# Moving the split of u in front of a drive in the gate stage of a hybrid RG-LRU / HGRN2 layer

## The chip, the cores and the metric

The kernel runs on one core of one Trainium2 chip. The metric is the device time of one execution in microseconds (us); a run's time is the median of several executions. Five engines work side by side, each through its own instructions in a fixed order, and wait for each other by semaphores: PE (TensorE, matmuls), ACT (ScalarE), DVE (VectorE), POOL (GpSimd) and SP (which issues most DMAs).

## What is computed

One layer for 512 latent tokens and 256 context tokens, 2048 wide. A normalised, modulated input h is multiplied by one wide input matrix. Its columns feed two groups, a gated linear recurrence (RG-LRU, 16 blocks of 128 channels) and a HGRN2 group; both outputs, gated, go through an output matrix. Only the RG-LRU group is touched by the change. For each block:

```python
ua = dwconv_centred(xa, conv_w, conv_b)            # 4 taps
r = sigmoid(ua @ w_r + b_r)                        # per block, per direction
i = sigmoid(ua @ w_i + b_i)
log_a = -8.0 * r * softplus(-lam)
a = exp(log_a)
bx = sqrt(-expm1(2.0 * log_a)) * (i * ua)
h = linear_scan(a, bx, h0)                         # context first, then latent
ya = (h_fwd + flip(h_bwd)) * silu(ga)
```

## The kernel before

The input product is made in units of 128 columns: h stands still in SBUF as 16 pairs of tiles (a rounded part `h` and its remainder, both in a format that PE takes at full rate), and the weights stream through `wraw`, six buffers deep. For each weight block ACT rounds it into `whi` (line 146), POOL makes the remainder `wlo` (line 147), and PE multiplies `whi` with both parts of h and `wlo` with the first (`mm_unit`, lines 204, 205 and 207). Five buffers of `whi` and `wlo` stand between ACT, POOL and PE.

The first stage, up to about 630 us, makes the columns of the RG-LRU group, two units per block of channels: xa and ga. Here a block of 128 channels is called a head, h = 0 to 15. The elementwise work and the gate products of a head are cut into small steps that stand in a queue `wq`; after every second weight slice of the main product a credit decides whether the next one or two steps are written into the program. So the order of all instructions on every engine is fixed when the program is built.

`steps_a(h)` (from line 357) makes the 13 steps of a head, in two lists, `first` and `second` (lines 457 and 458):

- `conv_a`, `conv_b`: the convolution of four taps into `u`; the first tap on ACT (line 369), the others on DVE (line 371). `u` has one buffer, so the first tap of the next head waits until POOL has read the last one's u (line 416).
- `split`: ACT rounds u into `uh` (line 390), and DVE subtracts, `ul = u - uh` (line 391).
- `g2(0)`, `g2(1)`: for each direction two gate products on PE (lines 402 and 403, six matmuls each, of `uh`, `ul` and `uh`), into two PSUM banks per product out of four banks `w`; then two sigmoids on ACT (lines 406 and 407) into the tiles `r` and `i`. `g2(0)` takes all four banks, and so `g2(1)` waits on PE until ACT has read them.
- `tanh`: two activations on ACT, and the product i*u on POOL, in place (line 416, twice).
- `exp`, `sqrt`: two activations each on ACT (lines 420 and 424), each pair behind a load of an activation table.
- `drive(d)`: two DVE instructions on `s` for direction d (lines 429 and 430); the first needs the square root of that direction.
- `scan(d)`: two scans on DVE (lines 439 and 441), over context (`hc`) and latent tokens (`hl`), which read `r` of the direction, now holding a.
- `fin`: the sum of both directions and the product with the gate on DVE, and the DMA of the result.

`r` and `i` have two buffers each, one per direction. So a sigmoid of `g2(0)` of head h overwrites the buffer that `scan(0)` of head h - 1 reads, and waits for that scan.

`push_a` puts the steps of a head together with the second list `p` of the preceding head. Written by their names, the order before is: conv_a(h), exp(h-1), conv_b(h), sqrt(h-1), drive(0)(h-1), split(h), scan(0)(h-1), drive(1)(h-1), scan(1)(h-1), g2(0)(h), fin(h-1), g2(1)(h), tanh(h). Where the text says "the cycle of head h", it means these 13 steps.

Of the kernel before, what the change touches and what calls it, by code (L numbers as in the profile page):

```python
# [56 lines left out]
def layer_kernel(ctx: ExitStack, tc, xT, xres, w0, w0e, wi, adas, adag, adagb, wo, par, lw, fw, cst, masks, out):  # L57
# [405 lines left out]
    def push_a(h):  # L463
        f, n = steps_a(h)
        if prev:
            p = prev.pop()
            f = [f[0], p[0], f[1], p[1], p[2], f[2], p[3], p[4], p[5], f[3], p[6], f[4], f[5]]
        wq.extend(f)
        prev.append(n)
        if h == NH - 1:  # L470
            wq.extend(prev.pop())
# [5 lines left out]
    e, a, n2, s2, p, m = (sm[:, i, :] for i in range(6))  # L477
# [45 lines left out]
    for h in range(2):  # L523
        evac_ga(h, PG[h])
        push_a(h)
# [337 lines left out]
    for i in range(NP):  # L863
# [13 lines left out]
        if i < 4 * NA:  # L877
            u, g = divmod(i, 4)
            cb = ORDER_A[u]
            full = cb < 16  # L880
            if g == 0:
                ph = psm.tile([128, 2, 512], F32, name="m")
            for k in range(4):
                mm_unit(ph if full else ph[:, 1, :], hi[:, k, :], lo[:, k, :], 4 * g + k, full)
                if k % 2:
                    credit += 1.5 if full else 1.0
                    while credit >= 1.33:
                        credit -= 1.33
                        run_steps(1)
            if g == 3:  # L890
                if cb >= 16:
                    evac_ga(cb - 16, ph[:, 1, :])
                else:
                    evac_xa(cb, ph[:, 0, 0:C], ph[:, 1, :])
                    push_a(cb)
            continue
# [190 lines left out]
```

## Time and profile before

| what | value |
|---|---|
| median of 3 runs | 2274.55 us (2274.06 to 2274.7) |
| the profiled execution, its own time | 2273.24 us |
| its span in the trace | 2271.5 us |
| PE busy | 2238.4 us, 99% of the span |
| DVE busy | 1233.7 us, 54% |
| ACT busy | 1014.5 us, 45% |
| POOL busy | 954.4 us, 42% |

Busy time says how long an engine had an instruction in it; it does not say what that engine waited for, nor that the others have room at each moment. The trace gives for each instruction its start, its duration and, in square brackets, how long its engine stood idle ahead of it and which instruction ended that idle time. A duration can hold a wait too: an instruction that has started but cannot get at its data is shown as long.

### The profile page before, as it was taken

The numbers are of one execution on the slowest core, as the hardware profiler recorded it, in microseconds if no ns is written. First come the engines' busy times: TensorE is split into PE (matmuls) and PEld (weight loads), VectorE is DVE, ScalarE is ACT, GpSimd is POOL, SyncE is SP. The second block draws the span as 40 slices with busy tenths as digits, with TensorE's granted clock in tenths as the row PEclk, the third lists the DMA queues.
The fourth block names the chain that finished last, engine by engine and source line by source line (L and its number), as shares of the span: only waits on it lengthen the run. The fifth ranks groups of instructions, "written<-read, shape, count | busy, mean of one in ns | idle before, by whom it ended". The sixth has DMA issues, their size and how long they took to land.

```text
span 2271.5 us, 40504 instructions
## 1 busy us (share of the span) xinstructions
PE 2238.4 (99%) x16318; PEld 1915.5 (84%) x16318; DVE 1233.7 (54%) x1834; ACT 1014.5 (45%) x1845; POOL 954.4 (42%) x698
## 2 busy tenths in 40 slices
PE   8999999999999999999999999999999999999998
PEld 4788888888898898898898898998998987788886
DVE  5447666665645666565576566556646647610011
ACT  4357767777634343343334334334334334422222
POOL 2355555565532433433333234234424334455452
PEclk9999999999999999999999999999999999999999
DMA  9942222222222323323223223223223224553443
GB/s 365 361 152 84 80 84 84 84 94 79 70 75 78 86 80 89 89 76 88 76 86 91 69 83 98 80 71 94 80 66 107 76 70 127 176 162 97 125 122 110
DMA packets 121396, 242.05 MB, mean 107 GB/s; under 512 B 13812, under 2 KB 16244, under 8 KB 121208
## 3 DMA queue, kind: packets, MB, share of 16 engines
q1 hardware_dynamic: 118520, 231.06, 32.9%
q0 software_dynamic: 2688, 8.40, 1.1%
q8 instruction: 128, 2.10, 0.4%
q14 instruction: 60, 0.49, 0.1%
HBM read 226.81 MB, written 12.59 MB: 105 GB/s over the span
## 4 chain that ended last, share of the span: by engine, by line
PE 92%; DVE 3%; issue 2%; ACT 2%; POOL 0%; DMA 0%; SPq 0%; ACTq 0%; DVEq 0%; POOLq 0%
PE m L205 22%; PE m L207 21%; PE m L204 12%; PE m L857 8%; PE w L975 8%; PE m L975 6%; PE w L857 4%; PE w L403 2%; PE w L685 2%; PE w L207 2%; PE w L769 2%; PE w L273 1%; PE w L402 1%; PE w L786 1%; PE w L785 1%
## 5 line engine op out<-in xcount | busy, mean ns | idle before, releaser
L147 POOL TENSOR_TENSOR wlo<-wraw,whi 128x512 fp32r<-128x512 f32 x556 | 793.4, 1437 | 1070.5 <-ACT whi L146 1013.6
L205 PE MATMUL m<-h,whi 128*128 128x512 f32 x1536 | 572.3, 395 | 0.0
L146 ACT CAST whi<-wraw 128x512 fp32r<-128x512 f32 x556 | 340.0, 620 | 457.2 <-issue 121.4
L207 PE MATMUL m<-h,whi 128*128 128x512 f32 x1440 | 448.1, 392 | 0.0
L204 PE MATMUL m<-h,whi 128*128 128x256 f32 x1536 | 437.9, 285 | 0.0
L205 PEld LDWEIGHTS m<-h,whi 128*128 128x128 f32 x1536 | 288.3, 188 | 63.7 <-issue 0.5
L207 PEld LDWEIGHTS m<-h,whi 128*128 128x128 f32 x1440 | 268.1, 188 | 55.8 <-issue 0.5
L205 PE MATMUL m<-h,wlo 128*128 128x512 f32 x768 | 303.6, 395 | 0.0
L204 PEld LDWEIGHTS m<-h,whi 128*128 128x128 f32 x1536 | 290.1, 189 | 8.9 <-issue 6.2
L207 PE MATMUL m<-h,wlo 128*128 128x512 f32 x720 | 280.9, 390 | 0.0
L204 PE MATMUL m<-h,wlo 128*128 128x256 f32 x768 | 216.2, 282 | 0.0
L857 PE MATMUL m<-whi,h 128*128 128x256 f32 x1024 | 207.8, 286 | 0.0
L658 DVE TENSOR_TENSOR KK<-KK,T 128x768 f32<-128x768 f32 x112 | 142.5, 1273 | 109.2 <-PE w L685 77.5
L205 PEld LDWEIGHTS m<-h,wlo 128*128 128x128 f32 x768 | 144.0, 188 | 35.1
L857 PEld LDWEIGHTS m<-whi,h 128*128 128x128 f32 x1024 | 168.5, 191 | 1.2 <-issue 0.2
L207 PEld LDWEIGHTS m<-h,wlo 128*128 128x128 f32 x720 | 135.2, 188 | 28.5
L590 DVE STREAM_TRANSPOSE ktok<-KK 32x384 f32<-32x384 f32 x256 | 145.9, 570 | 3.5
L371 DVE SCALAR_TENSOR_TENSOR u<-xp,P,u 128x256 f32<-128x256 f32 x96 | 88.2, 978 | 104.9 <-ACT u L369 104.9
L204 PEld LDWEIGHTS m<-h,wlo 128*128 128x128 f32 x768 | 145.0, 189 | 0.0
L857 PE MATMUL m<-wlo,h 128*128 128x256 f32 x512 | 144.8, 283 | 0.0
L638 ACT COPY Kc<-KK 128x512 f32<-128x512 f32 x80 | 54.6, 682 | 182.0 <-DVE KK L658 129.3
L776 DVE SCALAR_TENSOR_TENSOR S<-S,T,w 128x128 f32<-128x128 f32 x128 | 44.5, 348 | 134.9 <-ACT S L774 71.7
(222 smaller groups left out, 3762.1 us busy)
## 6 DMA issues: line engine op xcount, KB each, us to landing
wraw<-in_wi SPq DMA_DIRECT2D x428, 256.0 KB, 2.7
araw<-in_adas SPq DMA_DIRECT2D x64, 512.0 KB, 7.3
wraw<-in_wo SPq DMA_DIRECT2D x128, 256.0 KB, 2.7
wraw<-in_adag SPq DMA_DIRECT2D x64, 256.0 KB, 2.7
y_d<-ys POOLq DMA_DIRECT2D x32, 256.0 KB, 2.8
wraw<-y_d SPq DMA_DIRECT2D x32, 256.0 KB, 3.2
h<-in_xT SPq DMA_DIRECT2D x16, 384.0 KB, 7.4
wraw<-in_w SPq DMA_DIRECT2D x16, 256.0 KB, 7.9
```

The source lines that it names most:

```text
L146: act.copy(hi, t)
L147: pool.tensor_sub(lo, t, hi.bitcast(F32))
L204: pe.matmul(ph[:, 0, 0:C], w, h[:, 0:C], start=s, stop=e)
L205: pe.matmul(ph[:, 1, :], w, h[:, C:TA], start=s, stop=e)
L207: pe.matmul(ph, w, h[:, C:TA], start=s, stop=e)
L371: dve.scalar_tensor_tensor(dst, xp[:, o + k:o + k + n], cw, dst, op0=ALU.mult, op1=ALU.add)
L403: pe.matmul(pl, w[:, i, :], x[:, C:TA], start=n == 0, stop=n == 2)
L590: dve.transpose(dst[32 * j:32 * j + 32, :, 32 * i:32 * i + 32], src[32 * i:32 * i + 32, :, 32 * j:32 * j + 32])
L638: act.copy(Kc[l].rearrange("p c n -> p (c n)").rearrange("p (a b c) -> p a b c", b=2, c=m), view(s["K"], C, [[2 * m, C // m], [TA + m, 2], ...
L658: dve.tensor_mul(kk, kk, view(Tm, 1, [[2, nb // 2], [nb - 1, 2], [0, m]]))
L857: pe.matmul(o, x[:, 128 * j:128 * j + 128], wlin(w)[:, 256 * k:256 * k + 256], start=kb == 0 and n == 0 and j % 2 == 0, stop=kb == KB - 1 ...
L975: pe.matmul(pos[tk], y[:, 128 * tk:128 * tk + 128], wlin(x), start=(kb == 0 and n == 0), stop=(kb == 2 * KB - 1 and n == 2))
```

## The change

In `push_a` the step `f[2]` (split of head h) moves one place to the front, ahead of `p[2]` (drive of the first direction of head h - 1). Nothing is added or removed.

```diff
-            f = [f[0], p[0], f[1], p[1], p[2], f[2], p[3], p[4], p[5], f[3], p[6], f[4], f[5]]
+            f = [f[0], p[0], f[1], p[1], f[2], p[2], p[3], p[4], p[5], f[3], p[6], f[4], f[5]]
```

The order of the instructions on PE, POOL and SP stays the same. On DVE and ACT it changes as follows.

On DVE, in the cycle of head 7, ahead of the scan of the first direction (L371 are the taps of u, L429 and L430 the drive, L391 the remainder of u, L439 and L441 the scans). Before:

```order
L371 SCALAR_TENSOR_TENSOR u<-xp_1386,P,u 128x512
L429 SCALAR_TENSOR_TENSOR s<-r,s 128x768
L430 TENSOR_TENSOR s<-s,i 128x768
L391 TENSOR_TENSOR ul<-u,uh 128x768
L439 SCALAR_TENSOR_TENSOR hc<-r,s 128x256
L441 SCALAR_TENSOR_TENSOR hl<-r,hc,s 128x512
```

And now, at the same place:

```order
L371 SCALAR_TENSOR_TENSOR u<-xp_1386,P,u 128x512
L391 TENSOR_TENSOR ul<-u,uh 128x768
L429 SCALAR_TENSOR_TENSOR s<-r,s 128x768
L430 TENSOR_TENSOR s<-s,i 128x768
L439 SCALAR_TENSOR_TENSOR hc<-r,s 128x256
L441 SCALAR_TENSOR_TENSOR hl<-r,hc,s 128x512
```

The remainder of u stands ahead of both drive instructions now; this is so in the cycles of all heads from 1 to 15.

On ACT, in the cycle of head 7 (L424 are the square roots, L146 a weight block, L390 the rounding of u, L323 and L324 the evacuation of the next xa), as a difference of the two orders:

```order
 L424 ACT_TABLE_LOAD
 L424 ACTIVATE s<-s 128x768 x2
-L146 CAST whi<-wraw 128x512
-L390 CAST uh<-u 128x768
+L390 CAST uh<-u 128x768
+L146 CAST whi<-wraw 128x512
 L323 COPY xp_1386<-m 128x256
 L324 COPY xp_1386<-m 128x64x8
```

The rounding of u changes places with one weight block. On ACT this happens in the cycles of heads 1, 4, 5, 7, 8, 9 and 10; in the others the order of ACT is unchanged.

On DVE, in the cycle of head 10, with buffer numbers (gsa is the gate, which waits for a sigmoid of ACT):

```order
+L391 TENSOR_TENSOR ul_4190<-u_4128,uh_4189 128x768
+L354 TENSOR_TENSOR gsa_4195<-m_4097,sg_4193 128x512
 L429 SCALAR_TENSOR_TENSOR s_4104<-r_4019,s_4104 128x768
 L430 TENSOR_TENSOR s_4104<-s_4104,i_4030 128x768
-L354 TENSOR_TENSOR gsa_4193<-m_4097,sg_4191 128x512
-L391 TENSOR_TENSOR ul_4215<-u_4128,uh_4214 128x768
 L439 SCALAR_TENSOR_TENSOR hc_4230<-r_4019,s_4104 128x256
```

Here the drive now stands behind the gate product as well.

## Rows read from the trace of the kernel before

**Rows 1.** PE's waits, 200 to 640 us: us in total, times, longest.

```profile
PE w L402 <- DVE ul L391: 1.5, 3, 0.7
PE w L402 <- ACT r L406: 0.9, 1, 0.9
```

**Rows 2.** Waits of ACT, 130 to 640 us, same columns.

```profile
ACT r L406 <- PE w L402: 35.4, 11, 5.8
...
ACT u L369 <- POOL i L416: 30.8, 11, 4.5
...
ACT r L406 <- DVE hl L441: 22.0, 9, 4.5
ACT L406 <- DVE hl L441: 21.4, 6, 4.6
```

**Rows 3.** Timeline of ACT, head 7: start, us, instruction [idle before <-releaser].

```profile
354.35 1.58 ACT L424 ACTIVATE s<-s 128x768 f32<-128x768 f32 x2
355.83 0.61 ACT L146 CAST whi<-wraw 128x512 fp32r<-128x512 f32 x1
356.35 0.83 ACT L390 CAST uh<-u 128x768 fp32r<-128x768 f32 x1
...
363.12 1.28 ACT L406 ACT_TABLE_LOAD   x1 [3.75 <-DVE hl L441]
364.41 0.47 ACT L406 ACTIVATE r<-w,P 128x256 f32<-128x256 f32 x1
```

**Rows 4.** Timeline of DVE, head 7.

```profile
355.23 0.96 DVE L429 SCALAR_TENSOR_TENSOR s<-r,s 128x768 f32<-128x768 f32 x1 [1.83 <-ACT s L424]
...
357.21 1.94 DVE L391 TENSOR_TENSOR ul<-u,uh 128x768 fp32r<-128x768 f32 x1
...
360.88 2.14 DVE L441 TENSOR_TENSOR_SCAN hl<-r,hc,s 128x512 f32<-128x512 f32 x1
```

**Rows 5.** Timeline of POOL, head 7.

```profile
356.57 1.76 POOL L147 TENSOR_TENSOR wlo<-wraw,whi 128x512 fp32r<-128x512 f32 x1 [2.02 <-ACT whi L146]
358.99 2.95 POOL L147 TENSOR_TENSOR wlo<-wraw,whi 128x512 fp32r<-128x512 f32 x2 [0.66 <-ACT whi L146]
```

**Rows 6.** Timeline of PE, heads 7 and 15: first matmul of the second gates.

```profile
364.94 0.38 PE L402 MATMUL w<-uh,lhi 128*128 128x256 f32 x1 [0.94 <-ACT r L406]
...
604.79 0.28 PE L402 MATMUL w<-uh,lhi 128*128 128x256 f32 x1
```

**Rows 7.** Timeline of ACT, heads 3, 5 and 15.

```profile
238.39 0.83 ACT L390 CAST uh<-u 128x768 fp32r<-128x768 f32 x1
...
251.21 0.47 ACT L406 ACTIVATE r<-w,P 128x256 f32<-128x256 f32 x1 [3.77 <-PE w L402]
...
299.19 0.84 ACT L390 CAST uh<-u 128x768 fp32r<-128x768 f32 x1
...
603.69 0.47 ACT L406 ACTIVATE r<-w,P 128x256 f32<-128x256 f32 x1 [3.02 <-DVE hl L441]
```

**Rows 8.** Timeline of DVE, heads 3, 5 and 10.

```profile
237.28 0.96 DVE L429 SCALAR_TENSOR_TENSOR s<-r,s 128x768 f32<-128x768 f32 x1 [1.78 <-ACT s L424]
...
249.38 1.28 DVE L441 TENSOR_TENSOR_SCAN hl<-r,hc,s 128x512 f32<-128x512 f32 x1
...
296.37 0.96 DVE L429 SCALAR_TENSOR_TENSOR s<-r,s 128x768 f32<-128x768 f32 x1 [1.32 <-ACT s L424]
300.06 0.96 DVE L391 TENSOR_TENSOR ul<-u,uh 128x768 fp32r<-128x768 f32 x1 [1.74 <-ACT uh L390]
300.93 1.77 DVE L439 TENSOR_TENSOR_SCAN hc<-r,s 128x256 f32<-128x256 f32 x1
...
444.29 0.69 DVE L354 TENSOR_TENSOR gsa<-m,sg 128x512 f32<-128x512 f32 x1 [0.69 <-ACT sg L352]
...
446.93 1.77 DVE L439 TENSOR_TENSOR_SCAN hc<-r,s 128x256 f32<-128x256 f32 x1
```

## The prediction

> **What bounds the kernel now.** By the table of busy times PE is at work for 99% of the span, so only time in which PE stands idle can be won, and any new idle time of PE is lost. I looked first at what PE waits for in the gate stage, since the change lies there. In the sum of waits PE waits for ul, the remainder of u, in 3 places for 1.5 us, and for a sigmoid of the gates in one place for 0.9 us [rows 1]; no other line of that list is longer than half a microsecond. If the 2.4 us vanished, the kernel would gain 0.1%, less than the 0.2% that a measurement of it can tell from no change. The change can't win much; what has to be read is what it can lose.
>
> That is seen on the side of the other engines. The sum of ACT's waits has the sigmoids (L406, and the table load ahead of them) held by the scan hl of DVE 15 times, 43.4 us in all, and the first tap of u held by POOL's product i*u 11 times, 30.8 us; the 11 other waits of the sigmoids are for PE [rows 2]. Placed in time, nearly all the waits for PE lie in heads 0, 2 and 3 and again from head 11 on, and the waits for the scan lie in heads 4 to 10 and in 15. So from head 4 to head 10 the steps form a ring that hardly waits for PE: sigmoid, tanh, i*u on POOL, first tap of u, exp, square root, drive, scan, sigmoid of the next head. In these heads PE is the one who waits. Head 7 shows it: DVE starts the drive as soon as ACT has the first square root (355.23, after 1.83 us idle) and then works without a pause up to the end of hl at 363.02 (360.88 + 2.14) [rows 4]; ACT, idle for 3.75 us, loads its table at 363.12 and starts the sigmoid at 364.41 [rows 3]; PE had been idle for 0.94 us when the bank came free, and starts the second gates at 364.94 [rows 6]. A delay anywhere in that ring goes to PE, and the next head starts from there.
>
> **The change part by part.** No instruction is added or taken away, and no queue but those of DVE and ACT has another order; the DMAs of weights and results stay where they are. Two things move.
>
> First, the rounding of u goes ahead of one weight block on ACT in seven heads. It costs PE nothing by itself: that block comes 0.83 us later at most, the length of the rounding [rows 3], under the cover of the other buffers of whi, and no wait of PE for whi shows in this stage.
>
> Second, DVE does ul ahead of the drive. The drive needs only the first square root; ul needs both square roots and the rounding behind them on ACT. Before, DVE did the two drive instructions (0.96 us each) in just that time, and found uh ready [rows 4]. Now it stands idle. In head 7 the roots end at 355.93 (354.35 + 1.58), the rounding 0.83 later, at 356.76 at the latest [rows 3], where the drive had started at 355.23 [rows 4]. DVE's string of work is the same but starts 1.5 us later. Queued behind ul on DVE: drive and scan of the first direction, then of the second; for these wait the sigmoids, for them PE's second gates and the next head's u.
>
> What POOL does within that string is part of the price. The row of ul is 1.94 us, that of head 5 0.96 [rows 4, 8]; the long one began at 357.21, while POOL had its wlo open from 356.57 to 358.33 [rows 5]: the two took turns. The three wlo blocks of this stretch come as before or 0.8 us later, and POOL's next block starts at 358.99, within ul, and ends later than its own length: it gets in between two DVE instructions again [rows 5]. So I take it that the same wlo blocks still fall into the string, and give neither gain nor loss for them.
>
> Now head by head, each against before:
> - Head 3 brings the ring in late. Its rounding isn't moved and ends at 239.22 (238.39 + 0.83) [rows 7]; the drive had begun at 237.28, so the string starts 1.97 late, and the second hl, which ended at 250.66 (249.38 + 1.28), ends at 252.63 [rows 8]. The sigmoid that began at 251.21, waiting for PE [rows 7], now waits for that scan: +1.5.
> - Heads 4, 6, 7, 8, 9 show the pattern of head 7: +1.5 each, 7.5. (In 6 the rounding follows the roots already; in the others it does so now.)
> - Head 5: ul was waited for before, 1.74 us, until 300.06 [rows 8]. The rounding, one weight block (0.61 less their overlap of 0.1) earlier [rows 3], starts near 298.68 instead of 299.19 and ends near 299.52 [rows 7]; then ul 0.96, and the drive, 1.95, that used to lie in DVE's idle time: the scan starts near 302.45 instead of 300.93 [rows 8], +1.5; with one wlo block within the drive, 1.1 more. I take +2.0.
> - Head 10: the drive is now behind the gate gsa too, which waits for ACT's sigmoid; the rounding ahead of it puts gsa from 444.29 to about 445.04, its end at 445.73, and two drive instructions later it is 447.65 instead of 446.93 [rows 8]: +0.7, with a wlo block +1.8. I take +1.2.
> - Sum: 1.5 + 7.5 + 2.0 + 1.2 = 12.2. In heads 7 and 10 PE waited for the sigmoid before, so nothing is left to hide it: PE is 12.2 us late behind head 10.
> - Heads 11 to 14: the sigmoids wait for PE, 3.2 us on average over the 11 such waits [rows 2], and a string up to 1.97 late costs PE nothing. Head 1, which starts without a delay carried in, isn't in the sum either.
> - Head 15: as in head 3 the rounding isn't moved on ACT, and the string starts 1.97 late. The sigmoid ended at 604.16 (603.69 + 0.47), and PE came at 604.79, so 0.63 of it is covered [rows 6, 7]: +1.3. (The ring is not closed here; this head waits for the scan, but the heads ahead of it for PE.)
> - What is gained: the waits of PE for ul go, since ul comes 1 us earlier. But PE then only comes sooner to the second gates and waits there, in heads 5, 7 and 9, where these waits lay. I give it nothing.
>
> The sum is 13.5 us. Behind the gate stage PE has next to no idle time until the output product, and there it works at the same things as before: nothing gives the time back. Against the profiled execution's own time, 2273.24, this is 2286.7; the median of the runs is 1.3 above that execution, so 2274.55 + 13.5 = 2288.
>
> **The rivals.**
> *The ring catches up.* If a delay weren't carried from head to head (because something ahead of the first tap has room that the waits don't show), each head would pay for itself: 1.5 less its own cover. Heads 4 and 8 would pay nothing, 7 its full 1.5, 5 and 10 about 1.4 each, 15 its 1.3, 6 and 9 a few tenths each: about 6.5, so 2281. For it: a ring that waits for one thing only is rare. Against: the tap waits for POOL in each of these heads [rows 2].
> *DVE and POOL take turns otherwise.* ul now starts when no wlo is open, and runs 0.96 instead of 1.94; if the block that it used to wait for then fell behind the whole string, heads 1, 4, 7, 8 and 9, where the rounding passes one weight block, would each get 1.0 back: 13.5 - 4 or 5, so 2284 at the most and 2283 at the least. Against: in rows 5 POOL gets its turn between two DVE instructions. On this the Trainium skill, page "SBUF — State Buffer", section "Who interferes with whom", says that a DVE instruction with two inputs in SBUF and a GpSimd instruction that reads SBUF lock each other out, and that whoever issues first holds the shared ports for the whole instruction. The rows agree with turns of whole instructions; by that rule alone both orders of turns can come.
> *Not slower: PE covers the scan.* Place: the second gates. If the sigmoids were held by the gate products on PE and not by hl, the scan could come 1.5 us later unseen, and only the waits for ul would go: 2274.55 - 2.0 = 2272.5. It decides this from a cover of 1.5 us or more ahead of the second gates in heads 4 to 10, with nothing carried over. Against: [rows 2, 3, 6], where hl is the one that came last and PE was idle.
> *More than that.* If a wlo block more fell into the string in some heads, as bounded for 5 and 10 (1.1 each), it would be 2290 to 2292.
>
> **How the numbers follow.** Forecast, 2284.5 to 2291.5: 0.62. Turns otherwise, 2282 to 2284.5: 0.10. The ring catches up, 2279.1 to 2282: 0.12. More than 2291.5: 0.03. PE covers the scan, or the losses are below 0.2%: 0.11. Faster by over 0.2%, for which PE's idle time in this stage is too small: 0.02. The range from 2280 to 2291.5 leaves out the last three and a part of the third, 0.2 at most. Slower by over 0.2% (above 2279.1): 0.87; within 0.2%: 0.11; faster: 0.02.
>
> **What would show it.** In the profile after: DVE idle ahead of ul, released by uh, some 1.5 us longer in heads 3 to 10 than ahead of the drive now; the drive directly behind ul; PE's waits for ul gone, but its waits for the sigmoid ahead of the second gates in heads 4 to 10 and in 15 grown from about 1.3 to over 10 us in all, single ones of 1 to 3 us; the same main matmul 12 us later at 460 us, and 13 us later at 620. It would be wrong if these waits stayed under 5 us, or if the sigmoids in heads 5 to 9 waited for PE.

## The result

The changed kernel takes 2290.42 us (median of 4 runs, 2289.84 to 2292.41), the kernel before 2274.31 in the same comparison: a ratio of 1.0075, 95% interval 1.0057 to 1.0092. It is slower by 16.1 us; 13.5 were forecast (2288), and 2290.4 lies near the upper end of the range of 2280 to 2291.5.

The page of the profile after, span and PE's busy time:

```profile
span 2289.1 us, 40504 instructions
PE 2244.8 (98%) x16318; PEld 1918.5 (84%) x16318; DVE 1227.0 (54%) x1834; ACT 1014.9 (44%) x1845; POOL 965.6 (42%) x698
```

The span is 17.6 us longer, and PE's busy time only 6.4 us: the rest, 11.2 us, is new idle time of PE. What PE waited for in the gate stage, 140 to 660 us (us in total, times, longest):

```profile
PE w L402 <- ACT r L406: 11.4, 8, 2.6
PE w L403 <- ACT r L407: 1.6, 8, 0.2
PE w L402 <- DVE ul L391: 1.0, 2, 0.9
PE w L402 <- ACT uh L390: 0.8, 1, 0.8
```

Against [rows 1] (the kernel before has the same two sums in this wider window), the wait of PE's gate products for a sigmoid went from one place and 0.9 us to eight places and 11.4. The waits for ul only fell from 1.5 to 1.0. On the other engines, 130 to 660 us:

```profile
DVE ul L391 <- ACT uh L390: 53.8, 15, 5.5
ACT r L406 <- DVE hl L441: 35.3, 10, 6.4
ACT L406 <- DVE hl L441: 34.2, 6, 7.0
ACT u L369 <- POOL i L416: 32.9, 11, 4.8
```

DVE now waits for uh ahead of ul in all 15 cycles, and ACT waits for the scan for 69.5 us where it was 43.4 [rows 2]. The wait of the tap of u for the product on POOL has hardly changed (30.8 to 32.9 us): the product only passes the delay on.

Head 7 in the timeline of ACT, DVE, POOL and PE, as in [rows 3 to 6]:

```profile
359.95 1.58 ACT L424 ACTIVATE s<-s 128x768 f32<-128x768 f32 x2
361.44 0.82 ACT L390 CAST uh<-u 128x768 fp32r<-128x768 f32 x1
362.16 0.61 ACT L146 CAST whi<-wraw 128x512 fp32r<-128x512 f32 x1
...
370.31 1.28 ACT L406 ACT_TABLE_LOAD   x1 [5.33 <-DVE hl L441]
371.61 0.47 ACT L406 ACTIVATE r<-w,P 128x256 f32<-128x256 f32 x1
```

```profile
362.29 0.96 DVE L391 TENSOR_TENSOR ul<-u,uh 128x768 fp32r<-128x768 f32 x1 [3.29 <-ACT uh L390]
363.17 2.06 DVE L429 SCALAR_TENSOR_TENSOR s<-r,s 128x768 f32<-128x768 f32 x1
365.26 1.93 DVE L430 TENSOR_TENSOR s<-s,i 128x768 f32<-128x768 f32 x1
367.22 1.67 DVE L439 TENSOR_TENSOR_SCAN hc<-r,s 128x256 f32<-128x256 f32 x1
368.93 1.28 DVE L441 TENSOR_TENSOR_SCAN hl<-r,hc,s 128x512 f32<-128x512 f32 x1
```

```profile
362.91 1.50 POOL L147 TENSOR_TENSOR wlo<-wraw,whi 128x512 fp32r<-128x512 f32 x1 [2.74 <-ACT whi L146]
364.60 3.74 POOL L147 TENSOR_TENSOR wlo<-wraw,whi 128x512 fp32r<-128x512 f32 x2 [0.19 <-ACT whi L146]
```

```profile
372.13 0.38 PE L402 MATMUL w<-uh,lhi 128*128 128x256 f32 x1 [1.55 <-ACT r L406]
```

DVE stands idle for 3.29 us ahead of ul, where it stood 1.83 ahead of the drive [rows 4]: 1.46 us more, against 1.5 forecast. (In heads 4, 6, 8, 9 and 10 it is 1.44 to 1.47 more.) From its start to the end of the first hl its string takes 7.92 us (362.29 to 370.21), where it took 7.79 (355.23 to 363.02): the same work, started later. ul itself takes 0.96 instead of 1.94, but the two drive instructions 2.06 and 1.93 instead of 0.96 each. POOL's blocks of wlo, which lay across ul and the scans before [rows 5], lie across the drive now; in head 7 none fell out of the string. The section of the Trainium skill named above (page "SBUF — State Buffer", "Who interferes with whom") says that the one that issues first holds the shared ports for its whole instruction, while the other waits; the trace agrees with turns of that kind: ul is open when wlo starts at 362.91, so wlo takes 1.50 us, and the drive behind it, at 363.17, waits for wlo.

How late PE is, head by head (us): the start of the last product of `uh` and the remainder `llo` in the second gates (`g2(1)`; line 402), less the same start in the kernel before, less the difference at head 0 (-1.75 us for the changed kernel, whose trace comes into the stage that much earlier, with no instruction changed up to there; the granted clock fell to 0.50 for 3.4 us near 33 us in the trace of the kernel before, and not in this one):

| kernel | 1 | 3 | 4 | 5 | 6 | 7 | 8 | 9 | 10 | 14 | 15 |
|---|---|---|---|---|---|---|---|---|---|---|---|
| changed | 1.2 | 1.1 | 2.3 | 6.4 | 9.4 | 8.9 | 9.4 | 12.4 | 14.1 | 14.0 | 15.7 |
| heads 3 to 10 | 0 | 0 | 0.6 | 5.8 | 7.7 | 7.1 | 7.5 | 9.5 | 11.4 | 11.4 | 11.4 |
| head 4 alone | 0 | 0 | 0.5 | 1.6 | 1.6 | 1.5 | 1.5 | 1.5 | 1.5 | 1.5 | 1.5 |
| ACT's part alone | 0 | 0 | -0.2 | -0.4 | -0.2 | -1.6 | -1.5 | -1.6 | 2.6 | 2.5 | 2.5 |
| changed, second u | 0 | 0 | -0.2 | -1.8 | -1.1 | -3.2 | -3.2 | -4.1 | -4.0 | -4.1 | -2.5 |
| before, second u | 0 | 0 | -0.2 | -1.8 | -1.8 | -4.2 | -4.3 | -5.1 | -5.6 | -5.7 | -5.6 |

The first row is the changed kernel; the others are experiments below. The changed kernel loses all its time up to head 10, nothing in heads 11 to 14, and 1.6 in head 15: 15.7 us by the end of the gate stage.

### The profile page after: what moved, and what is told of

Read it like the earlier page. It is cut to its first block, busy times and chain, and to the rows that moved or that the text cites. A ratio compares the mean times of both kernels' runs of the same rounds, so it can differ in the third digit from the quotient of the medians.

```text
span 2289.1 us, 40504 instructions
## 1 busy us (share of the span) xinstructions
PE 2244.8 (98%) x16318; PEld 1918.5 (84%) x16318; DVE 1227.0 (54%) x1834; ACT 1014.9 (44%) x1845; POOL 965.6 (42%) x698
## 4 chain that ended last, share of the span: by engine, by line
PE 84%; DVE 6%; ACT 5%; issue 3%; POOL 2%; DMA 0%; SPq 0%; ACTq 0%; DVEq 0%; POOLq 0%
PE m L205 20%; PE m L207 18%; PE m L204 10%; PE m L857 8%; PE w L975 8%; PE m L975 6%; PE w L857 4%; PE w L685 2%; PE w L769 2%; PE w L207 2%; PE w L273 1%; PE w L403 1%; POOL i L416 1%; DVE s L430 1%; DVE s L429 1%
## 5 line engine op out<-in xcount | busy, mean ns | idle before, releaser
L147 POOL TENSOR_TENSOR wlo<-wraw,whi 128x512 fp32r<-128x512 f32 x556 | 805.2, 1457 | 1081.0 <-ACT whi L146 1019.8
L146 ACT CAST whi<-wraw 128x512 fp32r<-128x512 f32 x556 | 340.2, 620 | 468.3 <-issue 115.5
L371 DVE SCALAR_TENSOR_TENSOR u<-xp,P,u 128x256 f32<-128x256 f32 x96 | 88.2, 978 | 101.2 <-ACT u L369 101.2
```

Of the source, the lines that this page charges most:

```text
L146: act.copy(hi, t)
L147: pool.tensor_sub(lo, t, hi.bitcast(F32))
L371: dve.scalar_tensor_tensor(dst, xp[:, o + k:o + k + n], cw, dst, op0=ALU.mult, op1=ALU.add)
```

## The experiments

The theory: DVE's idle time ahead of ul starts its string of drive and scans later, and from head 4 to head 10 a closed ring of steps hands that on from head to head. Each experiment was compared with runs of the kernel before of its own session, whose median was 2274.0 or 2273.3 us. The rivals: the swap on ACT costs, other turns of DVE and POOL cost, or each head pays for itself.

**ACT's part alone.** The rounding stands where the change puts it; ul is made behind the drive, in one step with it. (Line 390 keeps the rounding; the subtraction becomes a step of its own, f[6].)

```diff
-            f = [f[0], p[0], f[1], p[1], p[2], f[2], p[3], p[4], p[5], f[3], p[6], f[4], f[5]]
+            f = [f[0], p[0], f[1], p[1], f[2], lambda f=f, p=p: (p[2](), f[6]()), p[3], p[4], p[5], f[3], p[6], f[4], f[5]]
```

> ACT's part of the change alone: the rounding of u stands where the change puts it, ahead of a weight block, but DVE makes ul behind the drive as before (in head 10 the drive also stands behind the gate product, as in the change). Theory (DVE idle ahead of ul starts the string late, and the ring of steps hands it on): the string starts with the first square root again, so 2273 to 2277, within 0.15% of before. Rival (the weight block that comes later on ACT, and POOL's remainder of it, hold PE or DVE up): most of the 16 us stays, 2286 to 2291.

Measured: 2278.26 us, ratio 1.0016 (1.0007 to 1.0026), 1.3 us above the range of the theory, and far below the rival's. The swap on ACT is not what costs: up to head 9 PE is even 1.6 us ahead of the kernel before. All of the loss within the gate stage, from 1.6 us ahead to 2.6 late, comes in one place, head 10. PE's waits, 140 to 660 us, and DVE's timeline there:

```profile
PE w L402 <- DVE ul L391: 4.3, 3, 3.1
PE w L402 <- ACT r L406: 0.3, 1, 0.3
```

```profile
442.78 0.69 DVE L354 TENSOR_TENSOR gsa<-m,sg 128x512 f32<-128x512 f32 x1 [6.18 <-ACT sg L352]
443.39 0.95 DVE L429 SCALAR_TENSOR_TENSOR s<-r,s 128x768 f32<-128x768 f32 x1
444.37 1.93 DVE L430 TENSOR_TENSOR s<-s,i 128x768 f32<-128x768 f32 x1
446.22 2.01 DVE L391 TENSOR_TENSOR ul<-u,uh 128x768 fp32r<-128x768 f32 x1
```

Here the drive, ready long before, stands behind the gate product, DVE is idle for 6.18 us, and ul comes last, 3.1 us too late for PE's first gates. This order of DVE, gate product, drive, ul, is in neither kernel: before, the drive came first, and with the change ul does. PE's granted clock fell to 0.50 for 3.4 us at the end of that wait, and from the first product of ul to the next main product PE took 3.2 us, where the kernel before took 1.8. So the loss in head 10 can't be put down to the swap on ACT alone.

**DVE's part alone.** ul ahead of the drive, the rounding still behind the weight block.

```diff
+            f = [f[0], p[0], f[1], p[1], lambda: None, lambda f=f, p=p: (f[2](), p[2]()), p[3], p[4], p[5], f[3], p[6], f[4], f[5]]
```

> DVE's part alone: ul ahead of the drive, but the rounding of u stays behind the weight block on ACT, where it was before. Theory: all of the loss stays, and since uh comes 0.5 us later in heads 4, 7, 8, 9 and 10, up to 2.5 us more: 2290 to 2293. Rival (ACT's swap costs): back to 2274 to 2277.

Measured: 2292.32 us, ratio 1.0075 (1.0061 to 1.0088), as much as the whole change. DVE's order carries the loss; moving the rounding forward saves little of it. In the trace PE is 15.5 us late behind head 10 and 17.1 behind head 15, 1.4 more than with the whole change, of the up to 2.5 that a later uh could add.

**The rounding twice.** The changed kernel with two equal roundings of u.

```diff
-            act.copy(uh, u)
+            [act.copy(uh, u) for _ in range(1 + (h > 0))]
```

> The changed kernel with the rounding of u done twice on ACT in heads 1 to 15, the same values: uh comes 0.75 us later. Theory: DVE's string starts 0.75 later once more, in heads 3 to 10 and in 15, 8 or 9 times 0.75, so 5.5 to 7.5 us above the changed kernel: 2296 to 2298. Rival (the loss comes from DVE and POOL taking turns differently and not from the idle time ahead of ul): within 2 us of the changed kernel, 2288 to 2292.

Measured: 2297.38 us, ratio 1.0097 (1.0083 to 1.011): 7 us above the changed kernel, as the theory said. By the trace PE is 24.0 us late at the end of the stage, 8.3 more than with the change. More idle time ahead of ul, with the same order of instructions on DVE and POOL, costs in proportion, which turns of DVE and POOL alone do not explain. (A part of the 8.3 is the clock of PE: it fell to half four times in the gate stage of this trace, and once in that of the changed kernel.)

**Only heads 11 to 14; only head 4; only heads 3 to 10.** The new order under a condition on h:

```diff
+            f = [f[0], p[0], f[1], p[1], *((f[2], p[2]) if 11 <= h <= 14 else (p[2], f[2])), p[3], p[4], p[5], f[3], p[6], f[4], f[5]]
```

> The change in the cycles of heads 11 to 14 alone. Theory: there the sigmoids wait for PE, and a string of DVE up to 2 us late is covered: no loss, 2272 to 2276, and PE has no wait for a sigmoid in these heads. Rival (each head that has the change pays about the same, 16 us over 15 heads): 4.3 us, 2277 to 2280.

Measured: 2274.97 us, ratio 1.0005 (0.9996 to 1.0014), and PE 0.1 us late at the end of the stage. The change is free in these heads, where PE sets the pace.

> The change in the cycle of head 4 alone. Its second gates had 1.7 us of cover ahead of them on PE in the kernel before. Theory (the ring hands the late start on): PE doesn't wait in head 4, but comes later from head 5 on, where the cover was 0.4 us: PE 1 to 1.5 us late from the second gates of head 5 to the end of the stage, 2274 to 2277. Rival (each head pays for itself): the 1.5 us are covered in head 4 and nothing shows in head 5 or behind it.

Measured: 2277.22 us, ratio 1.0011 (1.0002 to 1.002), 0.2 us above the range. PE is 0.5 us late behind head 4 and 1.6 behind head 5, in which nothing was changed, and stays 1.5 late to the end of the stage. So the delay is handed on. That PE wouldn't wait in head 4 was wrong by half a microsecond. In head 5 it shows where I had not looked for it, at the first gates, since uh itself comes later; PE there in this kernel, and then in the kernel before:

```profile
302.06 0.38 PE L402 MATMUL w<-uh,lhi 128*128 128x256 f32 x1 [1.52 <-ACT uh L390]
```

```profile
300.08 0.39 PE L402 MATMUL w<-uh,lhi 128*128 128x256 f32 x1 [0.43 <-ACT uh L390]
```

> The change in the cycles of heads 3 to 10 alone. Theory: this is the ring, and it holds 12 of the 13.5 us of the forecast; in the trace the gate stage of the changed kernel was 16 us longer, of which heads 1, 2 and 15 gave 2.8, so 10.5 to 13 here: 2284 to 2288. Rival (loss in proportion to the heads changed): 8 of 15, 8.5 us, 2281 to 2283.

Measured: 2287.82 us, ratio 1.0062 (1.0046 to 1.0077), PE 11.4 us late: heads 3 to 10 hold nearly three quarters of the 15.7 us, not the half that they have of the heads. By the medians it is 14.6 us; of the 3.2 us between the two, the trace has 2.4 in the output product (last section).

**A second buffer for u, with and without the change.** The first tap no longer waits for POOL's i*u of the preceding head. The buffers share the space of a tile of the next stage; `w0raw`, `w0hi` and `w0lo`, of the start, go from 3 buffers to 2.

```diff
-                st_["u"] = aw.tile([128, TA], F32, name="u")
+                st_["u"] = bq.tile([128, TA], F32, name="q", bufs=2)
```

> The changed kernel with the ring cut elsewhere: u gets a second buffer (in the space of a tile that the next stage uses), so the first tap of a head no longer waits for POOL's product i*u of the head ahead; for room three small buffers of the start go from 3 to 2. Theory (a closed ring hands the late start on from head to head): the waits of PE for the sigmoids shrink to under 3 us and the loss is gone, 2270 to 2277. Rival (each head pays its own late start, without being handed on): the waits in the gate stage stay, 2286 to 2291.

Measured: 2273.64 us, ratio 0.9995 (0.9986 to 1.0004): with the ring cut, the changed kernel is as fast as the kernel before. All of PE's waits in the stage, 140 to 660 us:

```profile
PE w L402 <- ACT r L406: 0.9, 1, 0.9
PE w L403 <- ACT r L407: 0.6, 3, 0.2
```

What is left is mostly head 15, 1.6 us.

> The kernel before with the second buffer for u (and the three small buffers of the start at 2), the change not in it. Theory: the ring is cut, so the waits of PE for ul and the sigmoids in heads 4 to 10, 3.3 us, go, and no other loss is there: 3 to 5 us faster than before, 2269 to 2271.5, and 2 to 3 us faster than the changed kernel with the same buffers. Rival (the second buffer helps only where the split stands in front): same as before, 2273 to 2276.

Measured: 2270.57 us (2269.01 to 2271.43, 11 runs), ratio 0.9987 (0.9978 to 0.9995): faster than both kernels. No wait of PE is left in the gate stage, and the sigmoids wait mostly for PE (waits of ACT, 130 to 640 us):

```profile
ACT r L406 <- PE w L402: 40.9, 15, 4.8
ACT L406 <- PE w L402: 20.3, 6, 4.8
...
ACT r L406 <- DVE hl L441: 13.2, 4, 3.7
```

In [rows 2] the scan held them for 43.4 us. With the second buffer in both kernels the change still costs 3.1 us (5.6 against 2.5 won by the end of the stage, and 3.1 by the medians), 1.6 of it in head 15; without the buffer it was 15.7.

## Why the prediction was right, and where it was off

*What bounds the kernel.* Right. PE sets the pace but for a ring of steps in heads 4 to 10; cutting the ring at a place that the change doesn't touch, the tap of u, takes away all but 3.1 us of the loss of 15.7.

*The start of the string.* Right in size: 1.46 us in head 7 against 1.5. Both the doubled rounding and DVE's part alone say that idle time ahead of ul is the cause.

*The swap on ACT.* Right that it costs nothing by itself, up to head 9; in head 10 the run meant to show it had another order on DVE too.

*POOL's turns.* Right in head 7, from which it was read: the wlo blocks stay within the string (7.92 us against 7.79). In head 3 it was wrong, as the next point shows.

*The terms of the sum.* The total was near, but not each term. What a cycle adds to the delay of the ring can be read on ACT: the end of the first square root of a cycle, less the same in the kernel before, and the growth of this difference from one cycle to the next (us; the sums are of the unrounded values):

| cycle of head | 1 | 2 | 3 | 4 | 5 | 6 | 7 | 8 | 9 | 10 | sum |
|---|---|---|---|---|---|---|---|---|---|---|---|
| prediction | 0 | 0 | 1.5 | 1.5 | 2.0 | 1.5 | 1.5 | 1.5 | 1.5 | 1.2 | 12.2 |
| heads 3 to 10 | 0 | 0 | 0.1 | 1.6 | 2.7 | 1.2 | 1.6 | 1.5 | 1.3 | 1.5 | 11.4 |
| changed | 1.6 | 0.1 | 0.2 | 1.6 | 2.7 | 1.2 | 1.6 | 1.4 | 2.2 | 1.5 | 14.1 |

Heads 4 and 6 to 10 come out as forecast, within 0.3 us, but for head 9 of the changed kernel. Three things were off.

The first is "Head 1, which starts without a delay carried in, isn't in the sum either": it adds 1.6 us. The prediction placed the waits for the scan in heads 4 to 10 and in 15, but two of the 15 lie in head 1 of the kernel before (3.08 and 0.61 us). Its cover (how long PE still had other work when the sigmoid was done) was not set against the 1.5 us, as that of head 15 was. ACT before:

```profile
187.42 1.28 ACT L406 ACT_TABLE_LOAD   x1 [3.08 <-DVE hl L441]
```

PE sees only 1.2 of it in head 1, but the ring comes into head 4 1.8 us later than in the kernel with heads 3 to 10 alone, and keeps this distance up to the cycle of head 9.

The second is "Head 3 brings the ring in late": it adds next to nothing. DVE in the kernel with heads 3 to 10:

```profile
239.20 1.47 DVE L391 TENSOR_TENSOR ul<-u,uh 128x768 fp32r<-128x768 f32 x1 [3.73 <-ACT uh L390]
...
248.99 1.28 DVE L441 TENSOR_TENSOR_SCAN hl<-r,hc,s 128x512 f32<-128x512 f32 x1
```

The string starts 1.92 us late, as forecast, but the second hl ends at 250.27, 0.39 us before its time in the kernel before (250.66 [rows 8]). The string is 2.3 us shorter, since less of POOL's work falls into it: the second drive's first instruction, 1.98 us before, takes 0.93, and the second hc 0.69 instead of 1.79. This is the mechanism of the rival "DVE and POOL take turns otherwise", in a head that it didn't name.

The third is TensorE's clock, which the sum doesn't have. In the changed kernel PE waits 1.66 us ahead of the second gates of head 9. Behind that its granted clock falls to half, 1.2 GHz, for 3.4 us; the matmuls of 512 columns take 0.63 us instead of 0.40, and a sigmoid of ACT has to wait for them. The stretch (us, PE busy, PEld busy, DVE, ACT, POOL, PEclk, DMA share, GB/s), and ACT:

```profile
433.70:437.10 3.40, 3.40 (x12) 2.90 (x11) 3.33 (x3) 2.55 (x6) 1.78 (x1) 0.51 0.00 0
```

```profile
436.56 0.47 ACT L406 ACTIVATE i<-w,P 128x256 f32<-128x256 f32 x1 [0.74 <-PE w L402]
```

In the kernel with heads 3 to 10 alone PE waited 1.67 us there, the clock stayed at 2.4 GHz, and head 9 added 0.9 us less. So the 2.7 us by which the changed kernel is later than that one behind head 10 (14.1 against 11.4) are 1.8 from heads 1 to 3 and 0.9 from the clock.

With 1.6 us in head 15, put at 1.3, the whole is 15.7 where the sum was 13.5. That it came so near is in part luck: head 3, put 1.3 too high, makes up for most of head 1, and heads 5 and 9 were each 0.7 too low.

*The waits for ul.* That nothing is won by them was right, but not that they all go: they fell from 1.5 to 1.0 us, because the ring brings uh later too, as in head 5 of the kernel with head 4 alone.

*The rivals.* "The ring catches up" is ruled out by head 4 alone, "Not slower" by the result, and "DVE and POOL take turns otherwise" is not the account of the heads it named (in head 7 the drive became long as ul became short), though it happened in head 3.

*Where it was read.* PE's waits for the sigmoid were to grow from about 1.3 to over 10 us, singly 1 to 3: they are 13.0 with the wait at L403, the longest 2.6. Some are shorter than 1, and one of the eight lies in head 1.

## What to carry to other kernels

An engine that is half idle can still be in a closed ring of waits; what counts is not its busy time but whether the engine that sets the pace waits for the ring or the ring for it, head by head. In such a ring an instruction that needs a later result costs time when it goes in front of one that can already run, and here that was paid again in each turn: a sum head by head needs the waits of every head, not of one. What helped most here was not an order but a second buffer at the one place where a turn waits for the one ahead.

## What was not expected of the hardware

In the traces the output product of the changed kernel, where nothing is changed, took 3 us more. The granted clock of TensorE, by stretches (columns as above), of the changed kernel:

```profile
1908.20:1915.00 6.80, 4.26 (x102) 3.19 (x102) 3.69 (x5) 1.42 (x3) 1.16 (x2) 0.50 0.68 199
1952.00:1956.00 4.00, 1.68 (x8) 1.05 (x6) 3.87 (x8) 1.36 (x3) 2.20 (x2) 1.00 0.56 174
1956.00:1962.80 6.80, 6.16 (x19) 5.23 (x20) 3.44 (x7) 0.78 (x2) 0.35 (x1) 0.50 0.74 235
```

and of the kernel before:

```profile
1896.40:1899.80 3.40, 3.40 (x66) 2.37 (x70) 0.98 (x2) 0.62 (x1) 0.00 (x0) 0.51 0.59 196
1938.00:1941.90 3.90, 0.94 (x5) 0.47 (x4) 3.75 (x8) 1.24 (x2) 2.00 (x2) 1.00 0.62 211
1941.90:1948.70 6.80, 6.80 (x38) 5.90 (x39) 4.42 (x10) 2.19 (x5) 1.30 (x1) 1.00 0.61 210
```

In both kernels PE stands idle twice here, for 3.5 us (from 1907.2 to 1910.7 in the changed kernel, from 1892.7 to 1896.2 before) and for 2.96 us (up to 1956.6 and 1941.9), and comes back. In the kernel before, the clock fell to 1.2 GHz for 3.4 us behind the first gap and stayed at 2.4 behind the second; in the changed kernel it fell for 6.8 us both times, while PE still stood idle. This doesn't go with the change: the trace of the kernel with two roundings is as that of before (the same stage within 0.1 us), and that of the kernel with heads 11 to 14 alone, whose gate stage is as before, lost 2.7 us there. What decides it no run here shows.

Of the 17.6 us between the two traces the gate stage is 15.7 and the output product some 3; against that stand the 1.75 us by which the changed kernel's trace came into the stage earlier. The medians, 16.1 apart, agree with the gate stage. The smaller differences of the experiments don't always: all traces but those of the kernel before and of the two roundings are 2 to 3 us longer in the output product than that of the kernel before. ACT's part alone and head 4 alone are 4.3 and 4.0 us slower by the medians, but 2.5 and 1.5 in the gate stage; so the account of the heads goes by the traces.

Within the gate stage the clock stays at 2.4 GHz in the traces in which PE waits little there (before, heads 11 to 14, head 4 alone, both with the second u). It falls to half, each time behind a wait of PE of 1.3 to 3.1 us or at its end, once in the changed kernel, with heads 3 to 10 and with ACT's part alone, twice with DVE's part alone and four times with two roundings; behind other waits of that length it stays. So a wait of PE cost more than its own time in some places here.
